# A bidirectional trunk layer: retention operands split two chunks at a time, a quarter of the value projection moved to the turn, residual rows in spent W_out tiles

## The chip, the cores and the metric

The kernel runs on one core of one Trainium2 chip. The time is that of one execution on the device, in microseconds; where several runs are given, it is their median. A core has five engines with a queue each, which work side by side and wait for one another through semaphores: PE (TensorE, matrix products, with PEld for its weight loads), DVE (VectorE), ACT (ScalarE), POOL (GpSimd) and SP (SyncE, which here issues the loads). Data lie in SBUF; matrix products land in eight PSUM banks, six under the name ps and two under pt.

## The reference

One encoder layer on 1024 tokens with 1024 features: a gated feed-forward half-step, a mixing step, a second feed-forward half-step, each with RMS norms around it. The mixing projects the normed tokens once, and runs two token mixers on the result:

```python
h = _swiglu(_rms_norm(x, ffn1_pre_norm[l]), ffn1_w_in[l], ffn1_w_out[l])
x = x + 0.5 * _rms_norm(h, ffn1_post_norm[l])
rq, rk, rv, rg, nq, nk, nv, g_ret, g_na = jnp.split(u @ w_in, points, axis=-1)
scores = jnp.einsum('bhnqd,bhnkd->bhnqk', qc, kc) * intra[None, :, None]
inner = jnp.einsum('bhnqk,bhnkv->bhnqv', scores, vc)
upd = jnp.einsum('bhnkd,bhnkv->nbhdv', kc * k_dec[None, :, None, :, None], vc)
def step(state, u):
    return chunk_dec * state + u, state
y_ret = (jax.nn.silu(rg) * y) @ w_ret_out
y_na = _neighborhood_attention(na_heads(nq), na_heads(nk), na_heads(nv), rel_bias) @ w_na_out
merged = jax.nn.sigmoid(g_ret) * y_ret + jax.nn.sigmoid(g_na) * y_na
```

The retention has 4 heads with keys of 128 and values of 256, in 8 chunks of 128 tokens, once forward and once backward; the two results are added. The neighbourhood attention has 8 heads of 64 on a 16 x 64 grid. All is float32.

## The kernel before

**Products.** Each float32 operand is split into a high part (ACT casts it, L62) and the rest (DVE subtracts, L63), and each product is three matmuls: high by high (L94), high by low (L95), low by high (L96). So each weight tile costs ACT a cast and DVE a subtraction before PE can use it. Raw weights land in the tile wraw (128 x 1024, 512 KB, four buffers, loaded by SP, L73), their parts in wh and wl (eight buffers each). A load waits until what last lay in its wraw buffer has been read.

**The order of work.** The program is written as one sequence, and a scheduler orders each engine's queue from it. Where one stage leaves PE waiting, the code takes steps of a later one as filler: an object named fill runs a generator, and fill(n) takes n steps of it, three matmuls each. Three tables say how many: FLIP_FILL for the turn, NA_FILL for the neighbourhood attention, RET_FILL for the retention.

**The turn.** ffn_out ends the first FFN: seven Strassen-like products of four token blocks each (a11, s1, s2, s3, a22, a12, s4). Its epilogue adds the residual rows (xload, one of eight token tiles each: x0 to x3 in spent W_out tiles, x4 to x7 in wraw buffers), norms twice (L674, L685) and stores the new rows. Each token tile is then turned by PE (a flip: eight transposes, L133) into the operands of the next products; for the last four tiles, DVE and ACT also form the sums and splits a22, s1, s2, s3 and s4 (L288 to L300). In between, the filler first() runs: vproj projects the tokens 0 to 511 on wnv (the values of the neighbourhood attention: 8 k-steps x 4 token tiles = 32 steps, 96 matmuls), then mx.leads() runs the a11 and a12 products of the first three jobs (24 steps, 72 matmuls). The job phase behind it makes queries, keys and gates, starting with an s2 product. Two of the four wnv tiles are loaded ahead of the output stage (the dictionary ahead).

**Attention and retention.** products() is the filler of both: vproj on wrv[0] and wrv[1] (the values of the retention, two halves of 512 columns, in token groups of 3, 3 and 2; 64 steps each, 24 weight splits each), then the gates (a sigmoid at the end, L1422) and the output projection of the attention. In na_cores each of 32 units has scores (L932), an exp on ACT (L937), transposes and the values' product; NA_FILL gives 12 steps ahead of the first unit and two times two per unit. ret_cores handles a head at a time: backward through the chunks for the states sb (update, L1116), then forward chunk by chunk: scores times the decay (L1129) and its split, the value chunk's split (vget), the splits of the backward state (sb) and the forward state (st), the products, a norm (L1141 to L1147), and two chunks later the transposes and the gate (store, L1156, L1157). RET_FILL's entries n[0] to n[8] stand at its fill calls; n[5] is taken once per chunk.

Of the kernel before, what the change touches and what calls it, by code (L numbers as in the profile page):

```python
# [11 lines left out]
F32 = mybir.dt.float32  # L12
F32R = mybir.dt.float32r
AF = mybir.ActivationFunctionType
ALU = mybir.AluOpType
# [4 lines left out]
P = 128  # L20
# [8 lines left out]
NHP = 4  # L29

NA_FILL = (12, 2, 2)
RET_FILL = (14, 2, 2, 4, 2, 3, 0, 1, 2)
FLIP_FILL = (8, 8, 8, 8, 2)
LOADS = (6, 9, 12, 15, 18, 22, 28, 33, 38)
NA_UNITS = ((0, 0, 0), (3, 1, 0), (1, 0, 1), (1, 0, 2), (4, 1, 1), (4, 1, 2), (2, 0, 3), (5, 1, 3))
KEY_OFF = (0, 8, 24, 32)
# [652 lines left out]
def ffn_out(c, tiles, q, blocks, w_out, gl, ep, tail, side={}):  # L689
# [3 lines left out]
    nc = c.nc  # L693
# [3 lines left out]
    later, rest, flips, xs = [], [], [], {}  # L697
# [8 lines left out]

    def xload(t):

        if t < 4 or ep.pre is None:
            tile = (tiles[0][1] + tiles[0][0])[t // 2]  # L710
            xs[t] = tile[:, t % 2 * 2:t % 2 * 2 + 2].rearrange("p k f -> p (k f)")
            nc.sync.dma_start(xs[t], ep.resid(t))
        else:
            xs[t] = c.raw(ep.resid(t))


    order = []
# [105 lines left out]
    for n, (i, k) in enumerate(steps):  # L823
# [11 lines left out]
        if later and i > 3:  # L835
            f = later.pop(0)
# [224 lines left out]
def ret_cores(c, pool, spool, d, dec, fill, n):  # L1061


    nc = c.nc
    NC = TT
# [16 lines left out]
    def vchunks(h):  # L1082
        vraw = {}

        def get(cc):
            if cc not in vraw:
                c0 = cc // 2 * 2
                vr = pool.tile([P, 2, 256], F32, tag="vraw", name="vraw", bufs=3)
                nc.sync.dma_start(vr, d["rv"][c0:c0 + 2, :, h * 256:(h + 1) * 256].rearrange("c p d -> p c d"))
                vraw[c0], vraw[c0 + 1] = vr[:, 0], vr[:, 1]  # L1090
# [32 lines left out]
    def scores(h, ops, cc):  # L1123
        cs = slice(cc * P, (cc + 1) * P)
        sc = c.bank()[:, :P]
        c.mm3(sc, [o[:, cs] for o in ops["k"]], [o[:, cs] for o in ops["q"]], True, True)
        a = pool.tile([P, P], F32, tag="a", name="a", bufs=2)
        ap = [pool.tile([P, P], F32R, tag=f"a{q}", name=f"a{q}", bufs=2) for q in "hl"]
        nc.vector.tensor_tensor(a, sc, dec.dm[:, h], ALU.mult)  # L1129
        c.split(*ap, a)  # L1130
        return ap

    def norm(h, cc, cross, inner):
        y = pool.tile([P, 256], F32, tag="y", name="y", bufs=2)
# [30 lines left out]
    for h in range(RH):  # L1165
        fill(n[1])
        half(0)
        kf, kb = kd
        sb = pool.tile([P, NC, 256], F32, tag="sb", name="sb", bufs=1)
        vget = vchunks(h)  # L1170
        for cc in range(NC - 1, 0, -1):
            update(h, 1, kb, cc, vget(cc), sb[:, cc] if cc < NC - 1 else None, sb[:, cc - 1])
            fill(n[2])
            if left and cc < NC - 1:
                store(*left.pop(0))
            if cc == NC - 2:
# [5 lines left out]
        v, sbs, st, sf = vget(0), state(sb[:, 0], "b"), None, None  # L1182
        fill(n[4])
        for cc in range(NC):
            b = scores(h, ops, cc + 1) if cc < NC - 1 else None
            if cc == NC - 1 and raw:
                kd, half = kdec(h + 1, raw["k"])
                half(1)
            fill(n[5])
            q = [o[:, cc * P:(cc + 1) * P] for o in ops["q"]]  # L1190
            nsf = None
            if cc < NC - 1:
                old, st = st, pool.tile([P, 256], F32, tag="st", name="st", bufs=2)
                update(h, 0, kf, cc, v, old, st)
                nsf = state(st, "f")
            cross, inner = c.bank(), c.bank()[:, :256]
            if cc < NC - 1:
                c.mm3(cross[:, 256:], q, sbs, True, True)
            c.mm3(inner, a, v, True, True)
# [11 lines left out]
            a, sf = b, nsf  # L1211
    for e in left:
        fill(n[8])
        store(*e)
# [3 lines left out]
def trunk_layer(ctx: ExitStack, tc, x, xt, g1a, w1i, w1o, g1b, gma, wmt, wnv, wrv, logits, dtab, rope, bias,  # L1218
                wro, wno, wmo, gmb, g2a, w2i, w2o, g2b, out):
    nc = tc.nc  # L1220
# [5 lines left out]
    c = Core(tc, const, wpool, psum, dram)  # L1226
# [3 lines left out]
    def dt(name, shape):  # L1230
# [49 lines left out]
    ep = pool(ep_stack, "ep1")  # L1280
# [3 lines left out]
    q = [p.tile([P, 4, 512], F32, tag="x", name="q", bufs=n) for p, n in ((ep, 2), (ep, 2), (spool, 8), (spool, 8))]  # L1284
    ahead = {}
# [12 lines left out]

    qk = []

    def vproj(src, groups, done):

        for toks in groups:
            banks = {t: c.bank() for t in toks}
            for k in range(KT):
                if k % 2 == 0:
                    w = ahead.pop(k // 2) if k // 2 in ahead else c.load_w(src[k // 2])
# [10 lines left out]
    evpool = []  # L1318

    def ev():  # L1320
        return evpool[0].tile([P, S], F32, tag="ev", name="ev", bufs=3)

    def done_nv(t, b):
        e = evpool[0].tile([P, 512], F32, tag="ev", name="ev", bufs=6 if len(evpool) == 1 else 4)
        nc.scalar.copy(e, b)
        c.store(d["nv"][2 * t:2 * t + 2].rearrange("r c d -> (r c) d"), e)

    def done_rv(j):
        def f(t, b):
            e = ev()  # L1330
            nc.scalar.copy(e[:, :512], b)
            c.store(d["rv"][t][:, j * 512:(j + 1) * 512], e[:, :512])
        return f


# [13 lines left out]
    for f, k in zip(rest, FLIP_FILL):  # L1349
        fill(k)  # L1350
        f = f()
# [57 lines left out]
    evpool[:] = [mix]  # L1409

    def gate(i, dst, halves=(0, 1)):

# [230 lines left out]
```

## Time and profile before

| | us |
|---|---|
| median of 3 runs (2255.41 to 2257.74) | 2256.15 |
| the profiled execution | 2254.28 |
| its span | 2252.5 |
| granted TensorE clock over the span | 0.994 |

The stages that the change touches lie at these times from the span's start: the last s4 product of the first FFN ends at 673.65 and the first job starts at 726.31; the first scores of the neighbourhood attention run at 1010.98; the retention fills about 1196 to 1440. A row of the profile names the engine, the line, the operation, the tiles (out<-in) and the count; a wait names what ended it. Engine shares in the page are averages over all stages, so the rows of a window say more than the page's first lines.

### The profile page before, as it was taken

What the parts mean: (1) busy time and instruction counts of PE and PEld (TensorE: products, weight loads), DVE (VectorE), ACT (ScalarE), POOL (GpSimd) and SP (SyncE); (2) the same over time, 40 slices, a digit from 0 to 9 for tenths busy, and PEclk for the clock granted to TensorE, in tenths of its full rate; (3) what the DMA queues carried; (4) which work ended last, traced back from release to release, by engine and by line L of the source; (5) the groups of instructions that cost most, each with busy time, mean ns of one, the idle gap of its engine ahead of it and who ended that gap; (6) DMA issues with size and microseconds to landing.
All of it is one profiled execution on the core that took longest, in us unless ns stands there. A gap on an engine that the chain in (4) does not pass through costs nothing.

```text
span 2252.5 us, 29976 instructions
## 1 busy us (share of the span) xinstructions
PE 2196.9 (98%) x10200; PEld 1824.7 (81%) x10200; DVE 1637.6 (73%) x2911; ACT 985.0 (44%) x2041; POOL 581.7 (26%) x756
## 2 busy tenths in 40 slices
PE   6899999999998999999999999999999999999998
PEld 5678888888786887888888888888887888888886
DVE  7898878765459857759885678553899887876444
ACT  5444434332345322249785665422544343433232
POOL 1121212158521112311101222111112121215942
PEclk9999999999999999999999999999999999999999
DMA  6354434497555555557665466686446443449865
GB/s 252 131 176 161 169 140 156 180 395 297 196 184 188 173 175 142 140 165 252 195 217 176 152 221 234 246 305 227 146 145 219 141 178 131 163 158 365 291 227 180
DMA packets 155464, 449.89 MB, mean 200 GB/s; under 512 B 19632, under 2 KB 50480, under 8 KB 153200
## 3 DMA queue, kind: packets, MB, share of 16 engines
q1 hardware_dynamic: 112800, 311.36, 40.9%
q0 software_dynamic: 42512, 136.62, 16.7%
q8 instruction: 81, 1.33, 0.2%
q14 instruction: 71, 0.58, 0.1%
HBM read 302.93 MB, written 149.17 MB: 201 GB/s over the span
## 4 chain that ended last, share of the span: by engine, by line
PE 82%; DVE 6%; ACT 4%; issue 4%; DMA 2%; POOL 2%; POOLq 0%; SPq 0%; DVEq 0%; ACTq 0%
PE ps L96 26%; PE ps L95 25%; PE ps L94 25%; PE pt L95 1%; PE pt L96 1%; PE pt L94 1%; POOL rstd L104 1%; ACT wh L62 1%; DMA wraw<-in_dram 1%; ACT s L937 1%; DVE wl L63 1%; DMA qraw<-nq 1%; DVE s L933 0%; PE pt L133 0%; ACT pth L62 0%
## 5 line engine op out<-in xcount | busy, mean ns | idle before, releaser
L63 DVE TENSOR_TENSOR wl<-wraw,wh 128x512 fp32r<-128x512 f32 x472 | 314.7, 683 | 61.0 <-ACT wh L62 60.7
L62 ACT CAST wh<-wraw 128x512 fp32r<-128x512 f32 x476 | 272.9, 618 | 159.3 <-PE ps L95 57.5
L94 PE MATMUL ps<-wh,g 128*128 128x512 f32 x548 | 214.1, 391 | 0.4 <-DVE tmp L231 0.4
L95 PE MATMUL ps<-wl,g 128*128 128x512 f32 x548 | 213.6, 390 | 0.0
L96 PE MATMUL ps<-wh,g 128*128 128x512 f32 x548 | 213.3, 389 | 0.0
L567 ACT ACTIVATE c<-c 128x512 f32<-128x512 f32 x88 | 55.4, 632 | 195.1 <-DVE c L532 101.6
L63 DVE TENSOR_TENSOR wl<-w,wh 128x512 fp32r<-128x512 f32 x77 | 77.0, 1018 | 86.2 <-ACT wh L62 86.0
L63 DVE TENSOR_TENSOR wl<-x,wh 128x512 fp32r<-128x512 f32 x77 | 79.7, 1051 | 75.1 <-ACT wh L62 73.7
L94 PEld LDWEIGHTS ps<-wh,g 128*128 128x128 f32 x548 | 102.9, 188 | 21.9 <-DVE tmp L231 0.7
L95 PEld LDWEIGHTS ps<-wl,g 128*128 128x128 f32 x548 | 102.9, 188 | 21.3 <-DVE wl L63 0.5
L96 PEld LDWEIGHTS ps<-wh,g 128*128 128x128 f32 x548 | 102.9, 188 | 21.3
L94 PE MATMUL ps<-a11h,wh 128*128 128x512 f32 x276 | 111.3, 403 | 7.7 <-ACT wh L62 7.7
L62 ACT CAST wh<-t 128x512 fp32r<-128x512 f32 x58 | 36.0, 621 | 184.0 <-DVE t L526 183.9
L96 PE MATMUL ps<-a11h,wl 128*128 128x512 f32 x276 | 109.6, 398 | 6.2 <-DVE wl L63 6.1
L95 PE MATMUL ps<-a11l,wh 128*128 128x512 f32 x276 | 109.9, 398 | 0.1
L96 PE MATMUL ps<-a22h,wl 128*128 128x512 f32 x280 | 109.1, 390 | 0.6 <-DVE wl L63 0.6
L94 PE MATMUL ps<-a22h,wh 128*128 128x512 f32 x280 | 109.7, 392 | 0.0
L94 PE MATMUL ps<-a12h,wh 128*128 128x512 f32 x276 | 108.7, 394 | 0.5 <-ACT wh L62 0.3
L95 PE MATMUL ps<-a22l,wh 128*128 128x512 f32 x280 | 109.1, 390 | 0.0
L95 PE MATMUL ps<-a12l,wh 128*128 128x512 f32 x276 | 107.5, 390 | 0.0
L96 PE MATMUL ps<-a12h,wl 128*128 128x512 f32 x276 | 107.5, 389 | 0.0
L94 PE MATMUL ps<-s2h,wh 128*128 128x512 f32 x232 | 91.8, 396 | 7.5 <-ACT wh L62 7.5
(427 smaller groups left out, 6287.2 us busy)
## 6 DMA issues: line engine op xcount, KB each, us to landing
wraw<-in_dram SPq DMA_DIRECT2D x204, 512.0 KB, 4.6
g<-g0s SPq DMA_DIRECT2D x44, 512.0 KB, 4.2
g<-g1s SPq DMA_DIRECT2D x44, 512.0 KB, 4.8
g<-g0a SPq DMA_DIRECT2D x33, 512.0 KB, 3.3
g<-g1a SPq DMA_DIRECT2D x33, 512.0 KB, 4.4
g0s<-gth POOLq DMA_DIRECT2D x44, 256.0 KB, 4.7
g0s<-cmb POOLq DMA_DIRECT2D x44, 256.0 KB, 3.7
g1s<-gth POOLq DMA_DIRECT2D x44, 256.0 KB, 4.7
```

What stands on the lines that cost most here:

```text
L62: self.done = [nc.scalar.copy(h, src).ins, (eng or nc.vector).tensor_tensor(l, src, hf, ALU.subtract).ins]
L63: (eng or nc.vector).tensor_tensor(l, src, hf, ALU.subtract).ins]
L94: mm(ps, a[0], b[0], start=start, stop=False)
L95: mm(ps, a[0], b[1], start=False, stop=False)
L96: mm(ps, a[1], b[0], start=False, stop=stop)
L104: self.nc.gpsimd.tensor_tensor(r[:, :n], ms, self.mhalf[:, :n], ALU.pow)
L567: nc.scalar.activation(gate[j], gate[j], AF.Silu)
L937: nc.scalar.activation(s[:, e], s[:, e], AF.Exp, bias=st[:, 2 + e:3 + e], accum_out=st[:, 4 + e:5 + e])
```

## The change

Four things are edited.

1. *Residual rows.* x4 to x7 of the first FFN's epilogue are loaded into two W_out tiles of the block b21, which has been used up by then, and no longer into wraw.
2. *Turn and filler.* first() now runs vproj(wrv[0]) for tokens 0 to 511 between the wnv products and the leads: 96 matmuls, four weight loads, eight splits, four copies and four stores. FLIP_FILL gives 12 steps per flip for 8. products() then has the tokens 512 to 1023 of wrv[0] only, in groups of two tiles (32 steps with 16 weight splits; before 64 with 24). NA_FILL stays, so the attention's 148 steps are now 96 of the value projection and 52 of the gates (before 128 and 20).
3. *Retention.* The value chunks are split in pairs (one cast and one subtraction of 512 columns for two of 256), the backward states too (new function states), and the scores of two chunks are formed in one bank, multiplied by the decay and split together. The tiles v and vraw have two buffers of two chunks (vraw had three).
4. *Filler of the retention.* n[5] falls from 3 to 2, so 32 steps (96 matmuls) fewer run there.

```diff
-RET_FILL = (14, 2, 2, 4, 2, 3, 0, 1, 2)
-FLIP_FILL = (8, 8, 8, 8, 2)
+RET_FILL = (14, 2, 2, 4, 2, 2, 0, 1, 2)
+FLIP_FILL = (12, 12, 12, 12, 2)
...
-        if t < 4 or ep.pre is None:
-            tile = (tiles[0][1] + tiles[0][0])[t // 2]
-            xs[t] = tile[:, t % 2 * 2:t % 2 * 2 + 2].rearrange("p k f -> p (k f)")
-            nc.sync.dma_start(xs[t], ep.resid(t))
-        else:
-            xs[t] = c.raw(ep.resid(t))
+        tile = (tiles[0][1] + tiles[0][0] if t < 4 or ep.pre is None else (None, None, *tiles[1][0]))[t // 2]
+        xs[t] = tile[:, t % 2 * 2:t % 2 * 2 + 2].rearrange("p k f -> p (k f)")
+        nc.sync.dma_start(xs[t], ep.resid(t))
...
-                vr = pool.tile([P, 2, 256], F32, tag="vraw", name="vraw", bufs=3)
+                vr = pool.tile([P, 2, 256], F32, tag="vraw", name="vraw", bufs=2)
...
-            v = [pool.tile([P, 256], F32R, tag=f"v{q}", name=f"v{q}", bufs=3) for q in "hl"]
-            c.split(*v, vraw.pop(cc))
-            return v
+                v = [pool.tile([P, 2, 256], F32R, tag=f"v{q}", name=f"v{q}", bufs=2) for q in "hl"]
+                c.split(*v, vr)
+                for j in range(2):
+                    vraw[c0 + j] = [q[:, j] for q in v]
+            return vraw.pop(cc)
...
+    def states(sb, cc):
+        n = min(2, NC - 1 - cc)
+        s = [pool.tile([P, 2, 256], F32R, tag=f"sb{q}", name=f"sb{q}", bufs=2) for q in "hl"]
+        c.split(*[q[:, :n] for q in s], sb[:, cc:cc + n])
+        return {cc + j: [q[:, j] for q in s] for j in range(n)}
...
+    def scores(h, ops, c0):
+        sc = c.bank()[:, :2 * P].rearrange("p (c t) -> p c t", c=2)
+        for j in range(2):
+            cs = slice((c0 + j) * P, (c0 + j + 1) * P)
+            c.mm3(sc[:, j], [o[:, cs] for o in ops["k"]], [o[:, cs] for o in ops["q"]], True, True)
+        a = pool.tile([P, 2, P], F32, tag="a", name="a", bufs=2)
+        ap = [pool.tile([P, 2, P], F32R, tag=f"a{q}", name=f"a{q}", bufs=2) for q in "hl"]
+        nc.vector.tensor_tensor(a, sc, dec.dm[:, h:h + 1].to_broadcast([P, 2, P]), ALU.mult)
         c.split(*ap, a)
+        return {c0 + j: [q[:, j] for q in ap] for j in range(2)}
...
-            b = scores(h, ops, cc + 1) if cc < NC - 1 else None
+            if cc % 2 and cc < NC - 1:
+                a.update(scores(h, ops, cc + 1))
...
-            if cc < NC - 2:
-                sbs = state(sb[:, cc + 1], "b")
+            if cc < NC - 2 and cc % 2:
+                sbs.update(states(sb, cc + 1))
...
-        yield from vproj(wnv, ((0, 1, 2, 3),), done_nv)
+        yield from vproj(wnv, ((0, 1, 2, 3),), done_nv, True)
+        yield from vproj(wrv[0], ((0, 1, 2, 3),), done_rv(0))
         yield from mx.leads()
...
-            yield from vproj(wrv[j], ((0, 1, 2), (3, 4, 5), (6, 7)), done_rv(j))
+            yield from vproj(wrv[j], (((4, 5), (6, 7)), ((0, 1, 2), (3, 4, 5), (6, 7)))[j], done_rv(j))
```

(The new argument of vproj lets only the first call take the weights in ahead; the copies of vproj's results take half tiles, half_ev.) Three places show how the queues move; in the rows, in_0 is x, in_7 the weights of the jobs, in_8 wnv and in_9 wrv.

**SP at the end of the first FFN.** Before, the last two wnv tiles (in_8) stand behind the stores of the new rows x1 out of the wraw buffers:

```order
L675 DMA x1_91<-wraw_5506 128x512 x2
L675 DMA x1_91<-wraw_5532 128x512 x2
L73 DMA wraw_5854<-in_8_dram 128x1024
L675 DMA x1_91<-wraw_5557 128x512 x2
L675 DMA x1_91<-wraw_5710 128x512 x2
L73 DMA wraw_5919<-in_8_dram 128x1024
L73 DMA wraw_5996<-in_7_dram 128x1024
```

Now all four stand together ahead of the whole output stage (its first weights are the x rows from in_4):

```order
L73 DMA wraw_5394<-in_8_dram 128x1024
L73 DMA wraw_5439<-in_8_dram 128x1024
L73 DMA wraw_5850<-in_8_dram 128x1024
L73 DMA wraw_5884<-in_8_dram 128x1024
L704 DMA x_3968<-in_4_dram 128x2048
```

and the residual rows stand between the loads of the activations g for the a12 products:

```order
L640 DMA g_5105<-g0a12_78 128x1024
L711 DMA x_3974<-in_0_dram 128x1024
L640 DMA g_5123<-g0a12_78 128x1024
L640 DMA g_5160<-g0a12_78 128x1024
L711 DMA x_3974<-in_0_dram 128x1024
L640 DMA g_5184<-g0a12_78 128x1024
L640 DMA g_5207<-g0a12_78 128x1024
L711 DMA x_3975<-in_0_dram 128x1024
```

The loads of wrv[0] follow later among the s4 products' g loads.

**DVE in the flips.** Before, two flips' sums (L288 to L300) follow each other, with the leads' weight split (wl from wraw_5996) behind them:

```order
L288 TENSOR_TENSOR cmb_5947<-a11h_5218,cmb_5946 128x512
L299 TENSOR_TENSOR cmb_5876<-a12h_5227,cmb_5876 128x512
L289 TENSOR_TENSOR cmb_5947<-cmb_5947,a11l_5219 128x512
L300 TENSOR_TENSOR cmb_5876<-cmb_5876,a12l_5228 128x512
L63 TENSOR_TENSOR a22l_5807<-pt_5952,a22h_5806 128x4x128
L294 TENSOR_TENSOR cmb_5957<-pt_5952,cmb_5946 128x512
L63 TENSOR_TENSOR s4l_5833<-cmb_5876,s4h_5832 128x4x128
L63 TENSOR_TENSOR s3l_5812<-cmb_5947,s3h_5811 128x4x128
L63 TENSOR_TENSOR s1l_5817<-cmb_5957,s1h_5816 128x4x128
L296 TENSOR_TENSOR cmb_5947<-pt_5952,cmb_5947 128x512
L63 TENSOR_TENSOR wl_6000<-wraw_5996,wh_5999 128x512
```

Now the splits of wrv[0] (wl from wraw_6064 and wraw_6134) stand in the flip's sums, one flip at a time:

```order
L294 TENSOR_TENSOR cmb_5916<-pt_5911,cmb_5905 128x512
L63 TENSOR_TENSOR wl_6067<-wraw_6064,wh_6066 128x512
L63 TENSOR_TENSOR s3l_5820<-cmb_5906,s3h_5819 128x4x128
L63 TENSOR_TENSOR s1l_5825<-cmb_5916,s1h_5824 128x4x128
L296 TENSOR_TENSOR cmb_5906<-pt_5911,cmb_5906 128x512
L63 TENSOR_TENSOR wl_6071<-wraw_6064,wh_6070 128x512
L63 TENSOR_TENSOR wl_6137<-wraw_6134,wh_6136 128x512
L63 TENSOR_TENSOR s2l_5829<-cmb_5906,s2h_5828 128x4x128
```

The leads' first split stands at the 813th row of DVE (before: the 814th); the product that wants it stands 96 matmuls later on PE.

**ACT in the attention's last third.** Before, one gate's sigmoid stands among the exps (L937), with a table load on either side:

```order
L967 COPY ot_10462<-ps_10742 64x8x16 x2
L1422 ACT_TABLE_LOAD
L1422 ACTIVATE ev_10666<-ps_10667 128x512
L937 ACT_TABLE_LOAD
L937 ACTIVATE s_10762,nast_10763<-s_10762,nast_10763 128x384 x2
L62 CAST pth_10793<-pt_10795 128x384
```

Now such pairs follow each other every other unit (the lines are 3 less above, 13 more below in the changed file); two of five:

```order
L1435 ACT_TABLE_LOAD
L1435 ACTIVATE ev_10248<-ps_10249 128x512
L934 ACT_TABLE_LOAD
L934 ACTIVATE s_10344,nast_10345<-s_10344,nast_10345 128x384 x2
L62 CAST pth_10383<-pt_10385 128x384
L62 CAST pth_10383<-pt_10391 128x384
L964 COPY ot_10026<-ps_10397 64x8x16 x2
L62 CAST vh_10528<-vraw_10527 128x512
L62 CAST wh_11081<-wraw_11079 128x512
L934 ACTIVATE s_10417,nast_10418<-s_10417,nast_10418 128x384 x2
```

Over the whole program ACT has 18 table loads (before 10).

More of the change, by code (lines that the diff above doesn't have):

```diff
@@ L1087, in get @@
                 c0 = cc // 2 * 2
-                vr = pool.tile([P, 2, 256], F32, tag="vraw", name="vraw", bufs=3)
+                vr = pool.tile([P, 2, 256], F32, tag="vraw", name="vraw", bufs=2)
                 nc.sync.dma_start(vr, d["rv"][c0:c0 + 2, :, h * 256:(h + 1) * 256].rearrange("c p d -> p c d"))
-                vraw[c0], vraw[c0 + 1] = vr[:, 0], vr[:, 1]
-            v = [pool.tile([P, 256], F32R, tag=f"v{q}", name=f"v{q}", bufs=3) for q in "hl"]
-            c.split(*v, vraw.pop(cc))
-            return v
+                v = [pool.tile([P, 2, 256], F32R, tag=f"v{q}", name=f"v{q}", bufs=2) for q in "hl"]
[3 more added lines that the diff above has]
+            return vraw.pop(cc)
         return get
@@ L1121, in state @@
         return s
[L1123 to L1129, printed above, removed]
+    def states(sb, cc):
[11 more added lines that the diff above has]
+        nc.vector.tensor_tensor(a, sc, dec.dm[:, h:h + 1].to_broadcast([P, 2, P]), ALU.mult)
         c.split(*ap, a)
-        return ap
+        return {c0 + j: [q[:, j] for q in ap] for j in range(2)}
     def norm(h, cc, cross, inner):
@@ L1181, in ret_cores @@
         a = scores(h, ops, 0)
-        v, sbs, st, sf = vget(0), state(sb[:, 0], "b"), None, None
+        v, sbs, st, sf = vget(0), states(sb, 0), None, None
         fill(n[4])
         for cc in range(NC):
-            b = scores(h, ops, cc + 1) if cc < NC - 1 else None
+            if cc % 2 and cc < NC - 1:
+                a.update(scores(h, ops, cc + 1))
             if cc == NC - 1 and raw:
@@ L1197, in ret_cores @@
             if cc < NC - 1:
-                c.mm3(cross[:, 256:], q, sbs, True, True)
-            c.mm3(inner, a, v, True, True)
+                c.mm3(cross[:, 256:], q, sbs.pop(cc), True, True)
+            c.mm3(inner, a.pop(cc), v, True, True)
             if cc > 0:
@@ L1210, in ret_cores @@
             fill(n[7])
-            a, sf = b, nsf
+            sf = nsf
     for e in left:
@@ L1299, in trunk_layer, with vproj @@
     qk = []
-    def vproj(src, groups, done):
+    def vproj(src, groups, done, begun=False):
         for toks in groups:
@@ L1306, in vproj @@
                 if k % 2 == 0:
-                    w = ahead.pop(k // 2) if k // 2 in ahead else c.load_w(src[k // 2])
+                    w = ahead.pop(k // 2) if begun and k // 2 in ahead else c.load_w(src[k // 2])
                     if k > 3 and qk:
@@ L1316, in vproj, with half_ev @@
                 done(t, banks[t])
-    evpool = []
+    evpool, mixing = [], "mixing"
     def ev():
         return evpool[0].tile([P, S], F32, tag="ev", name="ev", bufs=3)
+    def half_ev():
+        if evpool[-1] is mixing:
+            return ev()[:, :512]
+        return evpool[0].tile([P, 512], F32, tag="ev", name="ev", bufs=6 if len(evpool) == 1 else 4)
     def done_nv(t, b):
-        e = evpool[0].tile([P, 512], F32, tag="ev", name="ev", bufs=6 if len(evpool) == 1 else 4)
+        e = half_ev()
         nc.scalar.copy(e, b)
@@ L1329, in f @@
         def f(t, b):
-            e = ev()
-            nc.scalar.copy(e[:, :512], b)
-            c.store(d["rv"][t][:, j * 512:(j + 1) * 512], e[:, :512])
+            e = half_ev()
+            nc.scalar.copy(e, b)
+            c.store(d["rv"][t][:, j * 512:(j + 1) * 512], e)
         return f
@@ L1408, in trunk_layer @@
     mix.tile([P, 104], F32, name="pad")
-    evpool[:] = [mix]
+    evpool[:] = [mix, mixing]
     def gate(i, dst, halves=(0, 1)):
```

## The prediction

> **What bounds the kernel now.** I read the page first, for who is busy and what the chain that ended last runs through.
>
> ```profile
> span 2252.5 us, 29976 instructions
> PE 2196.9 (98%) x10200; PEld 1824.7 (81%) x10200; DVE 1637.6 (73%) x2911; ACT 985.0 (44%) x2041; POOL 581.7 (26%) x756
> PE 82%; DVE 6%; ACT 4%; issue 4%; DMA 2%; POOL 2%; POOLq 0%; SPq 0%; DVEq 0%; ACTq 0%
> ```
>
> TensorE is busy 98% of the span, and the change neither adds nor removes a matmul. Only PE's waits can be won: 2252.5 - 2196.9 = 55.6 us by the busy time. The question is where they lie, so I cut the span into windows around the three places that the change touches: the turn from the first FFN to the mixing, the neighbourhood attention and the retention.
>
> ```profile
> 673.65:726.30 52.65, 45.04 (x201) 35.42 (x200) 49.12 (x84) 28.73 (x58) 9.49 (x16) 0.97 0.56 188
> 690.00:695.00 5.00, 4.43 (x14) 0.66 0.29 102
> 1100.00:1150.00 50.00, 48.80 (x284) 42.29 (x283) 42.51 (x125) 40.99 (x112) 5.63 (x9) 1.00 0.69 224
> 1150.00:1200.00 50.00, 50.00 (x285) 43.60 (x284) 32.31 (x87) 36.33 (x88) 2.68 (x5) 1.00 0.56 184
> 1200.00:1250.00 50.00, 50.00 (x286) 43.76 (x285) 34.56 (x93) 29.92 (x81) 9.19 (x14) 1.00 0.45 148
> 1250.00:1300.00 50.00, 50.00 (x287) 43.62 (x287) 33.05 (x88) 30.13 (x82) 10.30 (x17) 1.00 0.54 170
> 1300.00:1350.00 50.00, 47.51 (x264) 40.45 (x263) 37.71 (x91) 34.34 (x86) 12.80 (x18) 1.00 0.69 222
> 1350.00:1400.00 50.00, 48.66 (x275) 41.70 (x274) 39.94 (x102) 29.49 (x80) 13.11 (x20) 1.00 0.70 230
> 1400.00:1440.00 40.00, 40.00 (x218) 34.47 (x217) 28.20 (x64) 20.51 (x48) 11.55 (x18) 1.00 0.65 228
> ```
>
> The columns are length, PE, weight load, DVE, ACT, POOL, clock, DMA (the second row has PE, clock and DMA only). **The turn** is the one bad place: from the last s4 product (673.65) to the first product of the job phase (726.31) PE has 201 matmuls and DVE is busy 49.12 of 52.65 us. The retention loses 2.49 + 1.34 = 3.8 us, all in heads 2 and 3. What should the turn have taken? The next rows give the pace when PE does not wait.
>
> ```profile
> 697.53 1.07 PE L94 MATMUL ps<-wh,a12h 128*128 128x512 f32 x4
> 679.09 1.03 PE L133 MATMUL pt<-ident,q 128*128 128x128 f32 x8
> 690.57 0.50 PE L94 MATMUL ps<-a11h,wh 128*128 128x512 f32 x1 [3.61 <-ACT wh L62]
> 717.12 0.50 PE L96 MATMUL ps<-a11h,wl 128*128 128x512 f32 x1 [3.34 <-DVE wl L63]
> 708.22 1.28 DVE L63 TENSOR_TENSOR wl<-wraw,wh 128x512 fp32r<-128x512 f32 x2
> 683.59 9.18 SPq L73 DMA_DIRECT2D wraw<-in_dram  x4
> SPq L73 <- DVE q L685: 6.4, 4, 2.4
> ```
>
> One 512-wide matmul lasts 0.39, so four that end after 1.07 start (1.07 - 0.39) / 3 = 0.2267 us apart; eight transposes at 0.27 each give 0.109. The turn's 168 wide matmuls (96 of the value projection, 72 of the leads) and 32 transposes need 38.1 + 3.5 = 41.6 us; they took 52.65, so **11.1 us** are lost. The two long gaps are 3.61 + 3.34 = 6.95 of it. Behind the first the granted clock is 0.66 of full speed for 5 us (second row above): 5 x 0.34 = 1.7 more. The other 2.4 are short waits.
>
> Each gap has its own cause. The first ends with ACT's wh, a weight cast: the weights of wnv[2] and wnv[3] were asked for only from 683.59 on, since SP stood (last row) on DVE's L685, which frees the wraw slots in which the residual rows x4 to x7 lie. The second ends with DVE's wl of the leads' weights: they stand in DVE's queue behind the flips' Strassen sums, at 0.60 us each (1.28 - 0.68).
>
> **The change, part by part.** *Turn.* The residual rows leave wraw for spent W_out tiles, and all four wnv weights are loaded before the FFN's output stage. The first gap and its slow clock lose their cause: -3.61 - 1.7 = -5.3. The second: 96 matmuls of wrv[0] come in between, 96 x 0.2267 = 21.8 us for PE, and DVE gets only 8 weight splits for them, 4.8 us. From the first L288 to the last flip's s2l the new order of DVE has 61 full-width rows (before 51): 61 x 0.60 = 36.6 us. Begun three splits later than now (684.9 + 1.8), that ends at 723; with some waiting I say 728. PE needs 673.65 + 41.6 + 21.8 = 737.0 to reach the job phase, so DVE has about 9 us to spare where it now is late. What is late next: within a flip DVE has 15 to 18 rows (9 to 10.8 us) against PE's 42 matmuls and 8 transposes (10.4 us). That is nearly even, and a pt bank that L296 has not released may cost about half a microsecond on each of four flips. I take 11.1 - 2 = **-9**; the ends are -5 (only the first gap goes) and -10.5.
>
> The turn's other edits cost nothing. The four residual loads now stand on SP right ahead of g0a12 loads, and queued behind each is one g load, for which PE waits; it has its own, later slot to wait for, and without that cover it would be late by the load's wait. The rv casts (4 on ACT) fit into 28.73 of 52.65 busy, the 4 stores into POOL's 9.49. The x1 stores must leave their tiles before s4h is written; SP issues them back to back once L674 is done, as now.
>
> The 21.8 us added here are taken from the retention (96 matmuls of filler fewer), so as PE work they cancel.
>
> *Neighbourhood attention.* The count of filler steps stays at 148, but 96 are now wrv products and 52 gates (before 128 and 20).
>
> ```profile
> 1012.76 0.50 PE L95 MATMUL ps<-wl,a12h 128*128 128x512 f32 x1 [0.45 <-DVE wl L63]
> 1173.45 1.28 ACT L1422 ACT_TABLE_LOAD   x1
> 1175.90 1.28 ACT L937 ACT_TABLE_LOAD   x1
> 1177.20 0.62 ACT L937 ACTIVATE s<-s,nast 128x384 f32<-128x384 f32 x1
> ```
>
> Each gate's sigmoid among the softmax's exps changes the activation table twice. The new ACT order has 11 such loads here after the first exp, the old one 3: 8 x 1.28 = 10.2 us more for ACT, all between 1100 and 1200, where it is busy 40.99 + 36.33 = 77.3 of 100. It would be 88: still room, and around the pair of loads that is there now PE loses nothing (50.00 of 50.00). At the start only 24 instead of 36 filler matmuls stand ahead of the first scores, 2.7 us less cover for the wl split that already costs 0.45. I take half a microsecond for each, **+1**, with 0 and +4 (one uncovered microsecond at each of the four new pairs of loads) as ends.
>
> The row at 1177.20 follows its load after 1177.20 - 1175.90 - 1.28 = 0.02 us. The Trainium skill, ScalarE: Activation LUTs, What ACT_TABLE_LOAD costs, adds a drain of 1.38 us to the 1.28, 2.66 us a switch, which speaks against this change: by it the eight would be 21.3 us, ACT 98.6 of 100. The load's length agrees with this trace, the drain does not show.
>
> *Retention.* Values, backward states and scores are split two chunks at a time.
>
> ```profile
> L63 DVE TENSOR_TENSOR vl<-vraw,vh 128x256 fp32r<-128x256 f32 x60 | 24.8, 419 | 5.0 <-ACT vh L62 5.0
> L63 DVE TENSOR_TENSOR wl<-wraw,wh 128x512 fp32r<-128x512 f32 x35 | 23.9, 688 | 13.5 <-ACT wh L62 13.4
> L63 DVE TENSOR_TENSOR sbl<-sb,sbh 128x256 fp32r<-128x256 f32 x28 | 11.5, 421 | 5.4 <-ACT sbh L62 4.9
> L63 DVE TENSOR_TENSOR al<-a,ah 128x128 fp32r<-128x128 f32 x32 | 9.3, 290 | 6.5 <-ACT ah L62 6.3
> L1129 DVE TENSOR_TENSOR a<-ps,dec 128x128 f32<-128x128 f32 x32 | 9.0, 282 | 5.3 <-PE ps L96 5.3
> 1326.99 0.76 DVE L63 TENSOR_TENSOR sbl<-sb,sbh 128x256 fp32r<-128x256 f32 x2
> 1316.33 0.41 PE L1156 MATMUL pt<-ident,yn 128*128 128x128 f32 x2 [1.09 <-DVE kdl L66]
> 1341.04 0.38 PE L94 MATMUL ps<-vh,ah 128*128 128x256 f32 x1 [1.11 <-DVE y L1141]
> 1369.17 0.63 PE L1103 MATMUL pt<-ident,kraw 128*128 128x128 f32 x4 [0.57 <-DVE kdl L66]
> 1375.94 0.41 PE L1156 MATMUL pt<-ident,yn 128*128 128x128 f32 x2 [0.72 <-DVE kdl L66]
> ```
>
> By the means, L1129 and al save 32 x 0.282 - 16 x 0.419 and 32 x 0.290 - 16 x 0.419 = 2.3 + 2.6; sbl, now 12 wide and 4 narrow, 11.8 - 9.9 = 1.9; vl, now 32 wide (a last single chunk is split as a pair), 25.1 - 22.0 = 3.1: 9.9 us together. Instructions overlap, so the means flatter it: two 256-wide ones end after 0.76, 0.34 us apart, a pair at 0.60 saves 0.08, and over 72 fewer instructions that is some 5 us. ACT's casts save about as much. Neither was on the path in heads 0 and 1. Against it stands the filler: n[5] falls from 3 steps to 2 in each of 32 chunks, so a chunk shortens by three matmuls, 0.68 us, and DVE's share rises. It was 173.5 of 240 us from 1200 to 1440, 72%; with 5 to 10 less of 218 it is 75 to 77%. So the waits in heads 2 and 3, all on DVE, lose 0.68 us of cover apiece; five of them would grow by 3.4, and DVE's saving takes some back. A pair's scores are issued at the start of the odd chunk ahead of it, some 4 us of PE before their use; multiply, cast and split take three 256-wide instructions of 0.42, 1.3 us, which leaves 2.7 us; where that is gone, the inner product waits, and behind it the rest of PE's queue. I take **+2**, with -3 (they go) and +5 (they grow, and as many new ones of 0.3 come) as ends. Two vraw buffers instead of three bring the value loads later by one pair; DMA is at 0.45 to 0.70 there, and I cost it at nothing; if its landing shows, a split waits on ACT and DVE behind it.
>
> **Sum:** -9 + 1 + 2 = -6 against the profiled execution's 2254.28 us (span 2252.5 and 1.8 around it): 2248.3. The median of the runs shown, 2256.15, lies 1.87 above that execution, so the forecast is **2250.2**. With all low ends, -10.5 + 0 - 3 = -13.5, it is 2242.7; with all high ends, -5 + 4 + 5 = +4, 2260.2.
>
> **The rivals.**
> - *The turn is won by half.* DVE's even load per flip holds PE, and only the first gap and half a microsecond go: -5 + 1 + 3 = -1, 2255. For it: 49.12 of 52.65 busy. Against it: the 9 us to spare.
> - *The table loads land on the path.* If ACT falls behind the softmax, all eight show: -9 + 0.5 + 10.2 + 2 = +3.7, 2259.9. Against it: 88 of 100. Were each load to hold ACT as long again without being recorded, 20.5 instead of 10.2, 2270; the 0.02 us above leaves that 2 in 100.
> - *The retention's period does not shrink* (slower). Its place is the forward pass of a head; the price is the filler taken out, 32 x 0.68 = 21.8 us of PE idling, if a chunk is paced by DVE and the state it hands on (L1116, cast, split, product). It decides from the point where a chunk's DVE rows take over 4 us: then -9 + 1 + 21.8 = +13.8, 2270. If only heads 2 and 3 do, half: +2.9, 2259. Against it: at the overlapped pace a chunk has five 256-wide rows (1.8 us, the fused ones a little longer), half of each pair's L1129, al (0.34 together), vl and sbl (0.6), and half a weight split (0.3), some 3.1 us; and nothing is lost in heads 0 and 1. For it: all waits there are on DVE.
> - *The change does not do what it says*: PE's first gap merely changes its releaser, to DVE's splits; that is the first rival's time.
>
> **How the numbers follow.** A measurement tells about 0.2%, 4.5 us, from no change: faster means under 2251.6, slower over 2260.7. The forecast case gets 0.60 (0.53 of it faster, the rest same), the half-won turn 0.15 (0.03 faster, else same), the table loads 0.10 (same but for 0.03), the retention 0.12 (half of it slower by over 0.2%, half same), anything else 0.03 (faster 0.01, slower 0.02). That makes faster 0.57, same 0.32, slower 0.11. The range 2243 to 2260 takes in the forecast's ends and the rivals of no change, and leaves the full retention case out.
>
> **What would show it.** Turn: no gap at the second half of the value projection and no clock under 0.95 there; the first job product about 737 - 726 = 11 us later than now, or more if flips wait (then a gap released by cmb, L296). Attention: 11 table loads with PE's busy share unchanged between 1100 and 1200. Retention: some 20 us shorter than now. It is wrong if PE waits over 8 us in retention heads 2 and 3, or if the turn still shows a gap over 2 us.

## The result, and the profile after

The changed kernel takes 2266.91 us in the median of 7 runs (2263.96 to 2268.91), the kernel before 2256.15 (7 runs, 2253.59 to 2261.37): a ratio of **1.0049**, 95% interval 1.0039 to 1.0058. It is slower by half a per cent, some 11 us, where 6 us less were forecast, and outside the range given. The profiled execution has a span of 2263.9 us, 11.4 more than before. Of the page, the busy time and the chain:

```profile
span 2263.9 us, 29887 instructions
PE 2201.9 (97%) x10200; PEld 1827.1 (81%) x10200; DVE 1633.7 (72%) x2839; ACT 991.8 (44%) x1993; POOL 581.4 (26%) x756
PE 80%; DVE 8%; issue 4%; DMA 3%; ACT 3%; POOL 2%; SPq 0%; POOLq 0%; DVEq 0%; ACTq 0%
```

The matmuls are the same 10200, and 11 us more lie between them. The windows say where (columns as in the prediction: length, PE, weight load, DVE, ACT, POOL, clock, DMA):

```profile
673.02:736.90 63.88, 63.55 (x297) 52.71 (x297) 60.29 (x130) 35.67 (x74) 13.32 (x20) 1.00 0.56 188
1000.00:1050.00 50.00, 43.03 (x196) 34.61 (x195) 28.22 (x67) 26.71 (x59) 4.65 (x7) 0.93 0.65 218
1100.00:1150.00 50.00, 48.88 (x289) 42.85 (x288) 46.51 (x131) 44.41 (x116) 6.16 (x8) 1.00 0.86 278
1150.00:1200.00 50.00, 50.00 (x297) 44.39 (x297) 33.25 (x105) 46.35 (x105) 1.61 (x3) 1.00 0.43 136
1250.00:1300.00 50.00, 47.87 (x273) 40.87 (x272) 34.95 (x79) 30.59 (x73) 11.63 (x19) 1.00 0.57 179
1300.00:1350.00 50.00, 44.70 (x256) 38.17 (x254) 38.59 (x81) 33.58 (x74) 12.85 (x20) 1.00 0.63 194
1350.00:1400.00 50.00, 48.62 (x277) 42.20 (x276) 39.04 (x87) 29.04 (x71) 14.20 (x21) 0.97 0.68 225
1400.00:1440.00 40.00, 38.02 (x220) 32.36 (x219) 28.91 (x70) 22.07 (x56) 12.38 (x19) 1.00 0.54 181
```

The turn is cured: PE works 63.55 of 63.88 us, at full clock, though DVE is as full as before. The attention's table loads cost nothing: PE has 98.9 of 100 us from 1100 to 1200 (before 98.8). What the turn won is lost twice over: through the whole retention, heads 0 and 1 included, and at the attention's start (43.03 of 50), where the kernel before has

```profile
1000.00:1050.00 50.00, 49.10 (x266) 41.86 (x265) 40.59 (x110) 38.57 (x97) 5.31 (x7) 1.00 0.78 252
```

Busy time hides short waits, so from here on I use one measure. The **loss** of a stretch is the sum, over its matmuls, of the time from one start to the next beyond the pace of a PE that does not wait: 0.2267 us for 512 columns, 0.179 for 384, 0.120 for 256, 0.109 for a transpose or 128. The matmuls are the same in all kernels here, so their paces sum to the same, some 2168 us, and the differences in loss are the differences in span, to some tenths; how the paces are rounded moves the whole-kernel figures together, by under 1 us. The stretches are by each profile's own time: the turn 650 to 750, the attention 1000 to 1100 and 1100 to 1200, the retention 1200 to 1450. By profile, in us:

| | turn | attention, first 100 | second 100 | retention | whole kernel |
|---|---|---|---|---|---|
| before | 11.1 | 3.0 | 3.3 | 7.7 | 65.1 |
| after | 0.7 | 13.2 | 3.1 | 20.4 | 76.4 |
| change | -10.4 | +10.2 | -0.2 | +12.7 | +11.3 |

**The attention's start.** The raw queries and keys (qraw, kraw) are loaded by SP, then split, then used by the first scores. Ahead of them SP loads the decay table (dec) and gate rows (rg). SP's rows of the kernel before (start, length of the issue; x4 is four loads):

```profile
989.41 0.33 SPq L1462 DMA_DIRECT2D dec<-dec  x1
994.66 2.41 SPq L885 DMA_DIRECT2D qraw<-nq  x4
997.17 0.53 SPq L898 DMA_DIRECT2D kraw<-nk  x1
```

and of the kernel after, with PE's two gaps and the clock behind the first:

```profile
1007.98 0.33 SPq L1475 DMA_DIRECT2D dec<-dec  x1
1013.19 2.41 SPq L882 DMA_DIRECT2D qraw<-nq  x4
1015.71 0.52 SPq L895 DMA_DIRECT2D kraw<-nk  x1
1023.41 0.69 PE L929 MATMUL ps<-k,qh 128*128 128x384 f32 x1 [4.58 <-DVE k L63]
1046.35 0.30 PE L948 MATMUL pt<-ident,s 128*128 128x128 f32 x1 [2.35 <-DVE s L938]
1024.00:1030.00 6.00, 6.00 (x18) 4.19 (x17) 3.71 (x9) 3.15 (x6) 0.00 (x0) 0.60 0.80 294
```

The job phase's last product ends at 1003.0 before and at 1013.4 after. So qraw was asked for 8.3 us ahead of it, and is now asked for 0.2 us ahead of it. In the compiled order qraw waits for a matmul that reads another tile in the same place: before, the last product of s3; after, the last of s4, the phase's very last; and dec, which stands ahead of it on SP, waits for the last s1 instead of s2. SP's issues agree with it: dec goes out at 989.41 behind an s2 product that ends at 989.4, qraw at 994.66 behind an s3 product that ends at 994.8. The last line is the clock behind the 4.6 us gap, 0.60 of full speed for 6 us; the matmuls there lose 2.9 us more. The first scores now come 10.0 us behind the phase's end (before 8.0), and only 24 filler matmuls, 5.4 us, stand in between (before 36, 8.2 us), as the prediction had counted. So the gap has two parents, the late load and the thinner cover.

**The retention.** Two of its gaps; what ACT and DVE did ahead of the second; and DVE's groups from 1217 to 1440:

```profile
1271.17 0.63 PE L1101 MATMUL pt<-ident,kraw 128*128 128x128 f32 x4 [1.22 <-DVE kdl L66]
1349.51 0.50 PE L94 MATMUL ps<-vh,ah 128*128 128x256 f32 x1 [3.87 <-ACT ah L62]
1343.20 0.62 ACT L62 CAST wh<-wraw 128x512 fp32r<-128x512 f32 x1 [2.57 <-DMA wraw<-in_dram]
1346.19 2.49 DVE L63 TENSOR_TENSOR wl<-wraw,wh 128x512 fp32r<-128x512 f32 x4
1348.60 0.42 DVE L1135 TENSOR_TENSOR a<-ps,dec 128x256 f32<-128x256 f32 x1
L63 DVE TENSOR_TENSOR vl<-vraw,vh 128x512 fp32r<-128x512 f32 x32 | 22.0, 687 | 16.2 <-ACT vh L62 16.0
L63 DVE TENSOR_TENSOR sbl<-sb,sbh 128x512 fp32r<-128x512 f32 x12 | 8.1, 687 | 2.1 <-ACT sbh L62 2.0
L63 DVE TENSOR_TENSOR al<-a,ah 128x256 fp32r<-128x256 f32 x16 | 6.8, 423 | 8.0 <-ACT ah L62 7.9
```

The counts are those forecast (32, 12, 16), the busy time falls, but DVE stands idle ahead of the paired vl for 16.2 us where it was 5.0: pairs wait longer for their casts. And the casts wait for the loads of the value chunks; ACT's waits from 1200 to 1450 (us in total, times, longest), first before, then after:

```profile
ACT vh L62 <- DMA vraw<-rv: 4.6, 3, 2.9
ACT vh L62 <- DMA vraw<-rv: 21.9, 8, 5.8
```

Counted by size, the matmuls of the retention that start over 0.3 us late went from 5 to 14, those between 0.1 and 0.3 from 7 to 31. One wait stands out, the second gap: ACT stood 2.57 us on a weight load of the filler; behind it DVE did splits of pairs and four weight splits, and only then the multiply (L1135) of scores that PE had finished near 1342. With the slow clock behind it (0.66 for 5 us) it costs 5.9 us by the loss, nearly half of the 12.7; the rest is spread in small waits.

### The profile page after: what moved, and what is told of

Same layout as the page of the kernel before. It is cut to its first block, busy times and chain, and to the rows that moved or that the text cites. A ratio compares the mean times of both kernels' runs of the same rounds, so it can differ in the third digit from the quotient of the medians.

```text
span 2263.9 us, 29887 instructions
## 1 busy us (share of the span) xinstructions
PE 2201.9 (97%) x10200; PEld 1827.1 (81%) x10200; DVE 1633.7 (72%) x2839; ACT 991.8 (44%) x1993; POOL 581.4 (26%) x756
## 4 chain that ended last, share of the span: by engine, by line
PE 80%; DVE 8%; issue 4%; DMA 3%; ACT 3%; POOL 2%; SPq 0%; POOLq 0%; DVEq 0%; ACTq 0%
PE ps L96 25%; PE ps L95 25%; PE ps L94 25%; PE pt L94 1%; PE pt L95 1%; PE pt L96 1%; DVE wl L63 1%; POOL rstd L104 1%; DMA vraw<-rv 1%; DMA ry<-rg 1%; PE ps L929 1%; PE pt L948 1%; PE pt L133 0%; DVE s L930 0%; POOL ry L69 0%
## 5 line engine op out<-in xcount | busy, mean ns | idle before, releaser
L94 PEld LDWEIGHTS ps<-wh,g 128*128 128x128 f32 x548 | 102.9, 188 | 21.8 <-DVE tmp L231 0.7
L96 PEld LDWEIGHTS ps<-wh,g 128*128 128x128 f32 x548 | 102.8, 188 | 21.5
```

The lines of the kernel that those rows point to most:

```text
L94: mm(ps, a[0], b[0], start=start, stop=False)
L96: mm(ps, a[1], b[0], start=False, stop=stop)
```

## The experiments

Two theories for the attention: **P**, the place of the raw tiles, through the residual rows' edit; **F**, the new token groups of the filler. Two for the retention: **A**, the pairs; **B**, the missing filler step. Their losses (us, as above), with the medians and the ratio to the kernel before on the same chip:

| | turn | attention, first 100 | retention | whole | median | ratio, 95% |
|---|---|---|---|---|---|---|
| e1_resid | 12.9 | 7.1 | 8.2 | 69.3 | 2259.25 | 1.0022 (1.0013 to 1.0031) |
| e2_place | 0.8 | 13.6 | 19.1 | 74.0 | 2266.65 | 1.0058 (1.0041 to 1.0075) |
| e3_single | 0.8 | 13.8 | 15.0 | 71.1 | 2261.85 | 1.0033 (1.0021 to 1.0045) |
| e4_pairs | 11.6 | 3.2 | 10.1 | 67.4 | 2258.76 | 1.0014 (1.0004 to 1.0025) |
| e5_fill2 | 13.2 | 3.9 | 21.5 | 81.2 | 2270.36 | 1.0067 (1.0049 to 1.0085) |
| e6_place | 0.7 | 6.3 | 19.3 | 68.7 | 2259.75 | 1.0021 (1.0011 to 1.0031) |
| e7_back | 0.8 | 13.9 | 25.4 | 81.3 | 2271.52 | 1.0078 (1.0063 to 1.0093) |
| e8_pt | 0.7 | 12.8 | 22.3 | 78.8 | 2267.64 | 1.0058 (1.0043 to 1.0073) |
| e9_half | 6.2 | 5.1 | 10.2 | 66.3 | 2254.51 | 1.0001 (0.9991 to 1.0010) |
| e10_full | 0.8 | 6.9 | 16.5 | 66.0 | 2255.12 | 1.0007 (0.9998 to 1.0016) |

The losses are of one profile each, and the clock moves them: the turn has the same code in the kernel before, e4_pairs and e5_fill2, and reads 11.1, 11.6 and 13.2. So a difference of 2 us in one column shows nothing by itself.

**e1_resid.** The kernel before, and of the change only xload:

```diff
-        if t < 4 or ep.pre is None:
-            tile = (tiles[0][1] + tiles[0][0])[t // 2]
...
-            xs[t] = c.raw(ep.resid(t))
+        tile = (tiles[0][1] + tiles[0][0] if t < 4 or ep.pre is None else (None, None, *tiles[1][0]))[t // 2]
...
```

> The kernel before with one edit of the change: the residual rows x4 to x7 in W_out tiles. Theory P (place): the s1 to s4 tiles of the job phase now take other slots, and so the loads of dec, qraw and kraw at the start of the attention wait for the last s1 and s4 products instead of s2 and s3; qraw is issued about 8 us later against the job phase's end, PE waits 2 to 4 us at the first scores and the first 100 us of the attention lose 5 to 7 us instead of 3.0. The turn's first gap and its slow clock go (-5), the second (3.3) stays. Time 2252 to 2256. Theory F (filler): the loss at the attention's start came from the changed groups of the wrv[0] products, which are not changed here: no new wait there, 2250 to 2252.

Measured: 2259.25, slower than before, and so over both expectations. The attention part went as P says; SP's rows and the turn's two gaps:

```profile
997.92 0.33 SPq L1459 DMA_DIRECT2D dec<-dec  x1
1003.13 2.41 SPq L882 DMA_DIRECT2D qraw<-nq  x4
691.28 1.11 PE L133 MATMUL pt<-ident,q 128*128 128x128 f32 x4 [3.41 <-ACT cmb L285]
715.59 0.79 PE L96 MATMUL ps<-a11h,wl 128*128 128x512 f32 x1 [4.44 <-DVE wl L63]
```

As in the changed kernel, qraw is asked for only 0.2 us ahead of the job phase's end (1003.3 here), the first scores come 10.1 us behind it, and the loss at the start rises by 4.1, with the filler's groups untouched. So the residual rows' edit alone moves the s tiles to other places. With all 36 filler matmuls as cover PE's wait ahead of the first scores is 1.95 us here, where the changed kernel has 4.58. The turn was a surprise: the weights are there, and the first gap is still 3.4 us long, now waiting for ACT's copy of a flip. The wait for the weights had covered a second one that ends as late. The edit by itself wins nothing at the turn. (That the loss there rises by 1.8 is within what the clock does.)

**e2_place.** The changed kernel; in the attention's pool the tiles that are needed late are placed first:

```diff
+    pts = [[pool.tile([P, 6, P], F32R, tag=f"pt{q}", name=f"pt{q}", bufs=2) for q in "hl"] for _ in range(2)]
+    ots[0] = pool.tile([P, 16, 64], F32, tag="ot", name="ot", bufs=2)
...
```

> The changed kernel, with the attention's tiles in another order in its pool (the transposed probabilities and the output tile first), so that qraw and kraw no longer lie over an s4 tile; dec still lies over s1. Theory P: qraw is issued right after the last s1 product, some 4 us earlier than in the changed kernel, the gap of 4.6 us at the first scores falls under 1 us, the one of 2.3 us at the transposes too, and the time falls by 6 to 9 us, to 2258 to 2261. Theory F: no difference, 2265 to 2268.

Measured: no gain, where P expected 6 to 9 us. The trace says why; qraw is issued at 1007.09, 4 us ahead of the phase's end, but the split queries now lie over the job phase's output buffers, and ACT waits for a store of these to land:

```profile
1019.28 0.42 ACT L65 ACTIVATE qh<-qraw 128x256 fp32r<-128x256 f32 x1 [3.06 <-DMA sn<-ev]
```

One wait was exchanged for another, so the run decides nothing between P and F.

**e6_place.** The same idea with each tile placed by what lies under it: dec and rg first in their pool, and the split queries and keys, which are not written before the phase's end anyway, over the s4 tiles:

```diff
+    qpre = [[pool.tile([P, 16, 16], F32R, tag=f"q{e}{p}", name=f"q{p}", bufs=2) for p in "hl"] for e in range(2)]
+    ots[0] = pool.tile([P, 16, 64], F32, tag="ot", name="ot", bufs=2)
+    kpre = [pool.tile([P, S], F32R, tag=f"k{e}", name=f"k{e}", bufs=2) for e in range(2)]
+    krs = [pool.tile([P, S], F32, tag="kraw", name="kraw", bufs=1)]
...
+    tabs = mix.tile([P, 536], F32, name="dec")
+    rgs = [mix.tile([P, 2, P], F32, tag="rg", name="rg", bufs=2) for _ in range(2)]
...
```

> The changed kernel with other places in the pools: dec and rg first in theirs, and in the attention's pool the split queries and keys and the output tile ahead of kraw and qraw. Now dec waits for nothing, qraw for the last s3 product (as in the kernel before), kraw for the last s1 product. Theory P (the place of the raw tiles delays their loads): qraw is issued about 8 us ahead of the job phase's end, the gap of 4.6 us at the first scores falls under 1.5 us, the loss in the attention's first 100 us falls from 13.2 to 4 to 6 us, time 2257 to 2260. Theory F (the filler's new groups): the loss stays over 10 us, time 2264 to 2268.

Measured: 2259.75, the first gap gone, the loss at the start 6.3 instead of 13.2:

```profile
1006.26 2.42 SPq L886 DMA_DIRECT2D qraw<-nq  x4
1040.03 0.30 PE L952 MATMUL pt<-ident,s 128*128 128x128 f32 x1 [2.25 <-DVE s L942]
1037.07 0.62 ACT L62 CAST vh<-vraw 128x512 fp32r<-128x512 f32 x1 [2.70 <-DMA vraw<-nvg]
```

With qraw 7.9 us ahead of the phase's end the first scores follow without a wait, so the places are worth 6.9 of the 10.2 us here. Not all of that is P alone: in e1_resid, with the old filler, the same late load costs 4.1; the rest needs the thinner cover as well, with which the gap grows to 4.6 us. Of the other 3.3 most is the gap in the second line, which the changed kernel has too: ACT stands on a value cast whose load came late, with the exp behind it. In SP's order that load follows weights of the new two-tile groups, which come twice as dense as one would need for four tiles; that this is the cause was read, not tried by itself. In e9_half below, whose groups have three tiles, the gap is not there.

**e3_single** and **e4_pairs** exchange the retention's code: the changed kernel with single chunks and n[5] = 2, and the kernel before with pairs and n[5] = 3.

```diff
-            if cc % 2 and cc < NC - 1:
-                a.update(scores(h, ops, cc + 1))
+            b = scores(h, ops, cc + 1) if cc < NC - 1 else None
...
```

> The changed kernel with the retention's splits by single chunks as before, n[5] = 2 as in the change. Theory A (pairs): the lumps of two chunks make PE wait; the loss in the retention falls from 20.4 us to 8 to 11, time 2255 to 2258. Theory B (filler): one filler step less per chunk makes PE wait; the loss stays at 17 to 24, time 2264 to 2270.

> The kernel before with the retention's splits by pairs alone, n[5] = 3 as before and no other edit. Theory A: the loss in the retention rises from 7.7 us to 14 to 20, time 2262 to 2268. Theory B: it stays at 6 to 10, time 2254 to 2258.

**e5_fill2** is the kernel before with n[5] = 2 alone:

```diff
-RET_FILL = (14, 2, 2, 4, 2, 3, 0, 1, 2)
+RET_FILL = (14, 2, 2, 4, 2, 2, 0, 1, 2)
```

> The kernel before with n[5] = 2 instead of 3 and no other edit; the 32 steps left over run at the end of the retention. Theory B (one filler step less per chunk makes PE wait): the loss in the retention rises from 7.7 us to 13 to 17, time 2260 to 2264. Theory B' (only the other phase of the filler in the changed kernel does): it stays under 10, time 2254 to 2257.

"Pairs" stands for all of the retention's edit, the two vraw buffers for three included; no run parts the two. Measured, as retention loss: single chunks 7.7 with three steps and 21.5 (e5) or 15.0 (e3, another phase of the filler) with two; pairs 10.1 with three and 20.4 with two. Both theories have a part, and B the larger one: the missing step costs 7 to 14 us, the pairs 2.4 with the full filler and 5.4 without. In the second figure the gap of 3.87 us has a large part: at the same place e3_single has 0.6 us of loss, the changed kernel 4.0 and its slow clock. And ACT's wait for the value loads goes with the pairs: 21.9 us in the changed kernel and 20.4 in e4_pairs, 6.4 in e3_single and 7.5 in e5_fill2. e3 lies between its two expectations, e4 just above B's; e5 is worse than B said. From the first transpose of the retention to the last, the kernel before takes 230.4 us, e5 221.0 and e3 215.6: taking out 21.8 us of filler shortens it by 9 to 15. Which waits these are, by PE's rows of e5 (us in total, times, longest):

```profile
PE ps L94 <- DVE y L1141: 5.3, 8, 0.9
PE ps L94 <- DVE ss L1145: 2.0, 1, 2.0
PE pt L1156 <- ACT yn L1147: 1.4, 1, 1.4
PE pt L1103 <- DVE rg L1157: 0.9, 3, 0.4
```

The products wait for the norm's sum y, from head 0 on; the kernel before has

```profile
PE ps L94 <- DVE y L1141: 1.3, 2, 1.1
```

**e7_back.** The changed kernel with the missing steps taken from the backward pass instead of the forward one:

```diff
-RET_FILL = (14, 2, 2, 4, 2, 2, 0, 1, 2)
+RET_FILL = (14, 1, 1, 4, 2, 3, 0, 1, 2)
```

> The changed kernel with n[5] back at 3 and the 32 steps taken from the backward pass instead (n[1] and n[2] 1 for 2). If the forward pass is where the missing step is felt: the loss in the retention falls from 20.4 to 9 to 13 us, time 2256 to 2260. If less filler costs as much anywhere in a head: 17 to 24 us, 2264 to 2270.

Measured: 2271.52, the loss 25.4. Less filler costs anywhere in a head, backward rather more (there PE waits for the value splits: ACT vh 3.3 us, DVE vl 2.8 in its rows).

**e8_pt.** The changed kernel with the scores in the pt banks:

```diff
-        sc = c.bank()[:, :2 * P].rearrange("p (c t) -> p c t", c=2)
+        sc = c.bank("pt", 2)[:, :2 * P].rearrange("p (c t) -> p c t", c=2)
```

> The changed kernel with the retention's scores in the two pt banks instead of the six ps banks. If PE waits for ps banks that the norm's DVE work has not released: the loss in the retention falls from 20.4 us by 4 or more, time 2260 to 2263. If it waits for the data of the products: no difference within 2 us, or more loss where the transposes want the pt banks.

Measured: no gain (22.3 against 20.4). Freeing a ps bank by this way does not help. The run tests the wait for y poorly, though: in the changed kernel PE's rows for it come to 1.1 us (5.3 in e5_fill2). By the code it would be a wait for a bank, since the products that wait do not read y, and L1141 reads a ps bank; no run shows it.

**e10_full** and **e9_half** are candidates: e6_place with single chunks; and the same with only half of the move to the turn, so that the retention gets 16 steps back (the lines by which e9_half differs from e10_full):

```diff
-RET_FILL = (14, 2, 2, 4, 2, 2, 0, 1, 2)
+RET_FILL = (14, 2, 2, 4, 2, 3, 0, 1, 2)
-FLIP_FILL = (12, 12, 12, 12, 2)
+FLIP_FILL = (10, 10, 10, 10, 2)
...
-        yield from vproj(wrv[0], ((0, 1, 2, 3),), done_rv(0))
+        yield from vproj(wrv[0], ((0, 1),), done_rv(0))
...
-            fill(n[5])
+            fill(n[5] - cc % 2)
...
-            yield from vproj(wrv[j], (((4, 5), (6, 7)), ((0, 1, 2), (3, 4, 5), (6, 7)))[j], done_rv(j))
+            yield from vproj(wrv[j], (((2, 3, 4), (5, 6, 7)), ((0, 1, 2), (3, 4, 5), (6, 7)))[j], done_rv(j))
```

> The changed kernel with the places of e6_place and single chunks in the retention, n[5] = 2: both side effects of the change's other parts undone, what is left is the turn and the filler. If the causes add: 76.4 us of loss less 7.7 (places) less 5.4 (pairs) = 63, that is the 65 of the kernel before within 2 us, time 2253 to 2258. If the pairs or the places only hid the lack of filler: 2260 or more.

> A candidate: the changed kernel with the places of e6_place, single chunks in the retention, and only tokens 0 to 255 of wrv[0] at the turn (48 matmuls, 16 steps; FLIP_FILL 10), so that n[5] is 3 in even and 2 in odd chunks. By the causes found so far: turn loss 1 to 4 us (before 11.1), attention's first 100 us 5 to 7 (before 3.0), retention 10 to 15 (before 7.7): 2250 to 2257, within 0.2% of the kernel before. If the retention's loss goes with the filler step by step, its loss is half way between 7.7 and the 15.0 of e3_single, 11 us.

Measured: 1.0007 and 1.0001, no difference from the kernel before. e10_full comes out as adding the causes says (66.0 of loss, 63 worked out), and no version was found that beats the kernel before. e9_half is as expected in the attention and the retention, but its turn loses 6.2 us instead of 1 to 4: half of the added matmuls leave a gap of 3.06 us, released by L296's cmb. With the places and the pairs undone, the turn's 10.4 us and the filler's 8.8 (16.5 less 7.7) are left, and a rest at the attention's start.

## Why the prediction was wrong

- **What bounds the kernel, and the pace:** right. No matmul was added, and the whole change lies in PE's waits.
- **Turn, -9:** right in size (-10.4, the end of its range); of the waits for L296 one appears, of 0.3 us. Its first part was wrong: "The first gap and its slow clock lose their cause" fails in e1_resid, where the gap stays with another releaser. The rival "the change does not do what it says" was true of that edit, with ACT's copy as the new releaser instead of DVE's splits. The 96 matmuls moved in did the work for both gaps; no run has them without the residual edit, so whether that edit is needed stays open. The rest of the working came out: DVE's last s2l ends at 724.3 (forecast 723, with some waiting 728), the first job product starts at 737.07 (737.0).
- **"The turn's other edits cost nothing"** is the first step that failed, and with it the attention's +1. I followed the residual rows' tiles up to s4h in the turn, and not to the end of the job phase, where pools that open later lie on the same memory. It cost 4.1 us by itself (e1_resid) and 6.9 of the attention's 10.2 with the thinner cover (e6_place). That cover was seen, 24 filler matmuls for 36, and priced at half a microsecond for the wl split; it counted against the load, which had become late.
- **Table loads:** 8 more as counted, ACT at 90.8 of 100 (forecast 88), no loss from them.
- **Retention, +2:** the second step that failed; it measured +12.7. I priced the missing cover at the five waits that the trace showed, 0.68 us each. With a step less in all 32 chunks, waits of under a microsecond came everywhere, heads 0 and 1 included (their loss rose from 1.2 to 7.1), and a pair's scores once came late, the wait that the prediction had named and left 2.7 us for: 5.9 us with its clock. Instead of some 20 us shorter the retention is 9.4 shorter. The rival named for it ("the period does not shrink") had the sign, with 0.12, and only part of the place: the backward pass suffers as well (e7_back). 12.7 of its 21.8 us came, over half, but some of these are the pairs'. Its test was wrong: DVE's rows per chunk (3.1 us, under 4) say nothing of a chain over PE, ACT, DVE and PE, and DVE is at 38.59 of 50 where PE waits most.
- **DVE's saving by pairs:** as counted, and worth less than nothing: e4_pairs loses 2.4 us with no other edit, and its median is 0.04 to 0.25% longer. The term put at nothing, two vraw buffers for three, is where a wait shows: ACT stands on value loads for 21.9 us instead of 4.6, and DVE's splits behind it. Whether the buffers do it or the larger lumps is not separated.

## What to carry to other kernels

Filler is not spare work: before a step of it is moved, ask what it covers there, even in stages where PE never waits now; here 21.8 us of filler taken from the retention gave back only some 9 to 15. A tile that gets another place in a ring can delay a load several stages later, through what lies over it; the waits of the loads at each stage's start, compared between the two compiled orders, show it without a run. And a gap's releaser is only the last of its causes: what ends just ahead of it is the next.

## What the runs showed of the hardware

Behind every gap of PE of 3.4 us or more, in all twelve profiles, the granted clock was lower: 0.50 to 0.70 over the next 5 us, with matmuls of 512 columns 0.427 us apart instead of 0.227. It adds 1.5 to 3.1 us of loss to the gap (2.9 to the 4.58 us gap of the changed kernel). Behind shorter gaps, from 1.9 us on, it went both ways. e4_pairs and e5_fill2 each have a gap of 3.3 us at the turn's end, and the 5 us behind it read

```profile
715.00:720.00 5.00, 4.61 (x20) 1.00 0.44 120
```

in e4_pairs and

```profile
716.00:721.00 5.00, 4.62 (x13) 0.66 0.51 121
```

in e5_fill2 (length, PE, clock, DMA). In e9_half a gap of 3.1 us left the clock at 1.00. A job product in the kernel before waits 2.39 us, and the 5 us behind it read

```profile
868.24 0.50 PE L96 MATMUL ps<-a11h,wl 128*128 128x512 f32 x1 [2.39 <-DVE wl L63]
868.20:873.20 5.00, 4.96 (x15) 0.66 0.82 145
```

The same product waits as long in all twelve profiles, 2.38 or 2.39 us, and slow matmuls follow it in eight of them. So the length of such a gap does not tell whether it costs 0.3 us more or 1.8, and two profiles can differ by that much without any cause in the kernel.
